# Changing the engine order of a seven-product matrix stage, and where two of its weight operands are made

## The chip, the cores and the metric

The kernel runs on one core of a Trainium2 chip. Five engines of the core work side by side, each through its own list of instructions in order: TensorE (PE, matrix products), VectorE (DVE), ScalarE (ACT), GpSimd (POOL, which here issues transfers and does little else) and SyncE (SP, which issues transfers). Engines wait for each other through semaphores. The metric is device time of one execution in microseconds; lower is better.

## The reference

Two layers of a bidirectional encoder run over 512 + 256 = 768 tokens with a model width of 1024. Each layer has a mixer, a gated convolution FFN and a small per-layer embedding. The change touches the first half of the FFN alone, in both layers:

```python
def _conv_ffn(x, w_up, conv_w, conv_b, w_down):
    u = x @ w_up
    up = jnp.pad(u, ((0, 0), (1, 1), (0, 0)))
    u = up[:, :-2] * conv_w[0] + up[:, 1:-1] * conv_w[1] + up[:, 2:] * conv_w[2] + conv_b
    a, gate = jnp.split(u, 2, axis=-1)
    return (a * jax.nn.gelu(gate, approximate=False)) @ w_down
```

`w_up` is 1024 x 5632: 22 blocks of 128 columns for `a` and 22 for `gate`.

## The kernel before

Everything is float32. A product of precision is made of three fast ones: each operand is split into a high part `hi` (ScalarE's copy to the matrix format) and a low part `lo = x - hi` (VectorE's subtraction), and the products hi*hi, hi*lo and lo*hi are added in PSUM.

For the first 4 of the 22 pairs (a block of `a` and its block of `gate`) the projection is done plainly (`proj`). The other 18 pairs go through `seven()`, a Strassen-like scheme: the 2 x 2 product of a pair's weight blocks A11, A12, A21, A22 with the halves of the input is made with seven products instead of eight. The seven weight operands, in the order in which TensorE uses them, are A11, S1 = A21 + A22, S2 = S1 + A11, S3 = A11 + A21, A12, S4 = S2 + A12 and A22. The input operands (B11, N1, N2, T3, B21, B22, N4) are made once a layer. I call one call of `seven()` "a seven", and the two stretches of 18 sevens "the seven-product stage" of layer 0 and of layer 1. Each product is 4 blocks x 3 parts = 12 matmuls of 128 x 384, so a seven has 84.

PSUM holds four accumulators a seven: x, z, y and v. TensorE writes A11 to x, S1 to z, S2 to y, S3 to v, then adds A12 to x, S4 to z and A22 to v. Before z may be written again by S4, VectorE must have read it: `u2 = y + q1` (L191, where q1 is ScalarE's copy of x, L184) and `g = z + u2` (L192; both go to the tile `ug`). VectorE also adds the results into the rows `us[0]` and `us[1]` (`u`, L1081), ScalarE copies one quarter (L1083).

After each product `after()` is called: `tick()` takes one step of the convolution and gate work of the pair before (`activate`: ScalarE's scalings L1028 and Gelu L318, VectorE's four taps L1031 and the last multiplication L1051), and `split_step()` takes one step of `split_pair`, which prepares the weights of the next seven, one operand in a step. Its loads of A21, A11, A12 and A22 come over SP's queue (L88, L89, L94; tiles `ra` and `rb`). The weight sums are made in place, in the tile that held A21 (called s) or A11 (called a), by adding transfers that GpSimd issues (`accum_op=ALU.add`): L128 makes S1 = A21 + A22 for the seven after the next, the three of L115 make S2 (`more(s, 0)`), S3 (`more(a, 2)`) and S4 (`more(s, 1)`). The splits are L110 (ScalarE, `hi`) and L111 (VectorE, `lo`); tiles `whi`/`wlo` hold S1, A11, S3 and S4, tiles `hs`/`ls` hold A12, S2 and A22. The tile that holds a and s (`ra`) has two buffers, so the loads of the seven after the next wait until S4 of the present one is split.

The order of instructions on each engine is not that of the source: a scheduler in the framework places them by its own estimate of when each is ready and of what is urgent, and the engines then run what was placed, in that order.

Of the kernel before, what the change touches and what calls it, by code (L numbers as in the profile page):

```python
# [9 lines left out]
F32 = mybir.dt.float32  # L10
F32R = mybir.dt.float32r
U8 = mybir.dt.uint8
AF = mybir.ActivationFunctionType
ALU = mybir.AluOpType
# [31 lines left out]
class Net:  # L46
# [51 lines left out]
    def split_pair(self, w):  # L98
        nc = self.nc
        src, a, s = self.ploads.pop(0)  # L100
        tiles = {}

        def parts(name, r, n, half):
            if n is None:
                hi, lo = (self.fp.tile([128, 512], F32R, tag=t, bufs=3, name=t) for t in ("hs", "ls"))
            else:
                if n not in tiles:
                    tiles[n] = [self.wp.tile([128, 1024], F32R, tag=t, bufs=2, name=t) for t in ("whi", "wlo")]
                hi, lo = [t[:, half * 512:(half + 1) * 512] for t in tiles[n]]
            nc.scalar.activation(hi, r, AF.Copy)  # L110
            nc.vector.tensor_tensor(out=lo, in0=r, in1=hi.bitcast(F32), op=ALU.subtract)  # L111
            w[name] = [(hi[:, c:c + 128], lo[:, c:c + 128]) for c in range(0, 512, 128)]

        def more(t, n):
            nc.gpsimd.dma_start(out=t, in_=src[n], accum_op=ALU.add)  # L115
        a12 = self.load_block(src[1])
        parts("S1", s, 0, 0)
        more(s, 0)
        yield
        a22 = self.load_block(src[3])  # L120
        yield
        parts("A11", a, 0, 1)
        more(a, 2)
        yield
        parts("A12", a12, None, 0)
        if self.ploads:
            after, _, t = self.ploads[0]
            nc.gpsimd.dma_start(out=t, in_=after[3], accum_op=ALU.add)  # L128
        yield
        parts("S2", s, None, 0)  # L130
        more(s, 1)
        yield
        parts("A22", a22, None, 0)
        yield
        parts("S3", a, 1, 0)
        yield
        yield
        parts("S4", s, 1, 1)
        if self.psrc:
            self.ploads.append(self.load_pair(self.psrc.pop(0)))  # L140
        elif len(self.psplits) == 1:
            self.sp += 1
            self.prep()
        yield
# [21 lines left out]
    def seven(self, c11, add):  # L166
        nc = self.nc
        X, W = self.X, self.pw.pop(0)

        def prod(bank, a, b, start):  # L170
            for n, ((wh, wl), (xh, xl)) in enumerate(zip(W[a], X[b])):
                for i, (w, v) in enumerate(((wh, xh), (wh, xl), (wl, xh))):
                    nc.tensor.matmul(bank, w, v, start=start and n == 0 and i == 0, stop=n == 3 and i == 2,  # L173
                                     skip_group_check=True)

        def after():
            self.tick()
            self.split_step()
        q1 = self.rp.tile([128, T], F32, tag="Rt", name="q1")[:, 0:HC]
        ug = self.rp.tile([128, T], F32, tag="sq", name="ug")  # L180
        u2, g = ug[:, 0:HC], ug[:, HC:T]
        x, z = self.mm()[:, 0:HC], self.mm()[:, 0:HC]
        prod(x, "A11", "B11", True)
        nc.scalar.copy(q1, x)  # L184
        after()
        prod(z, "S1", "N1", True)
        self.begin_split()
        after()
        y = self.mm()[:, 0:HC]
        prod(y, "S2", "N2", True)  # L190
        nc.vector.tensor_tensor(out=u2, in0=y, in1=q1, op=ALU.add)  # L191
        nc.vector.tensor_tensor(out=g, in0=z, in1=u2, op=ALU.add)  # L192
        after()
        v = self.mm()[:, 0:HC]
        prod(v, "S3", "T3", True)
        add(1, 1, v, g)
        after()
        prod(x, "A12", "B21", False)
        c11(x)
        after()  # L200
        prod(z, "S4", "B22", False)
        add(0, 1, z, u2)
        after()
        prod(v, "A22", "N4", False)
        add(1, 0, v, u2)
        after()

# [779 lines left out]
    def ffn(self, l):  # L989
        nc, tc, a = self.nc, self.tc, self.a  # L990
        with tc.tile_pool(name=f"f{l}", bufs=1) as fp, \
# [43 lines left out]
            def activate(j, u, negated):  # L1035
                act[j] = aslot(j, f"act{j}", F32)
                if negated:
                    c = self.hp.tile([128, AC], F32, tag="h6", name="cg")
                else:
                    c = self.rp.tile([128, AC], F32, tag="sq", name="cg")  # L1040
                gbias = conv[:, NF + j, 3:4]
                gate = conv_taps(c, u[1], *((nconv, j, gbias) if negated else (conv, NF + j, gbias)))
                lin = conv_taps(act[j], u[0], conv, j, conv[:, j, 3:4])
                next(gate), next(lin)
                yield 1
                for _ in gate:
                    yield 1
                self.other(c, c, AF.Gelu)
                for _ in lin:
                    yield 1  # L1050
                nc.vector.tensor_tensor(out=act[j], in0=act[j], in1=c, op=ALU.mult)  # L1051

            def run(gen):
                for _ in gen:
                    pass
# [5 lines left out]
            for j in range(NSTD):  # L1061
                for part in range(2):
                    n = 2 * j + part
# [5 lines left out]
                    for (c0, w), (uc, _) in zip(CH, ACOL):  # L1069
                        nc.vector.tensor_tensor(out=us[part][:, 1 + uc:1 + uc + w], in0=pj[:, c0:c0 + w],  # L1070
                                                in1=self.R[:, c0:c0 + w], op=ALU.mult)
                    if part == 1:
                        run(activate(j, us, False))
            self.drain()
            self.begin_split()
            for _ in range(6):
                self.split_step()
            for j in range(NSTD, NF):
# [6 lines left out]
                next(taps)  # L1085
                self.spawn(taps)
            self.drain()
            self.use_lnexp()
            for ph in range(2):
                accs = []  # L1090
# [7 lines left out]
                for j in range(NF):  # L1098
                    if j % 2 == 0:
                        hi, lo = self.slab()  # L1100
# [271 lines left out]
```

## Time and profile before

| | us |
|---|---|
| median of 3 runs | 2441.41 (2431.51 to 2442.25) |
| the profiled execution, its own time | 2439.16 |
| its span, first to last instruction | 2437.4 |
| seven-product stage of layer 0, from first product to the next stage's first | 332.87 |
| the same of layer 1 | 338.77 |

The profiled execution's time lies 1.8 us above its span (what lies around the instructions), and 2.3 us below the median of the runs. Stretches are given in us from the span's start. In the rows below PE is TensorE's matmul; a matmul's start is measured, its end is modelled, so the distance of starts is what counts; an instruction on another engine that is shown to take 0.69 us may be followed by the next 0.6 us after its start. "[3.49 <-DVE ug L192]" is idle time before the instruction and what ended it. The granted clock (PEclk) is the share of TensorE's full 2.4 GHz.

### The profile page before, as it was taken

Reading aid. Unit: us, or ns where it says so; the run is one execution under the profiler, and the core shown is the slowest. Engines: PE = TensorE matmul, PEld = TensorE weight load, DVE = VectorE, ACT = ScalarE, POOL = GpSimd, SP = SyncE. Lnnn points to the kernel's source line nnn. Section 1 sums busy time; section 2 is a strip of 40 time slices with the busy share of each in tenths; the row PEclk is TensorE's granted clock in tenths of the full one; section 3 lists DMA queues with packets and bytes.
Section 4 is the critical chain, followed back from the end, with each engine's and each line's share of the span. In section 5 each row is a group of like instructions: output and inputs, shape, how many; then the busy total and the mean of one; then the engine's idle time right before and its main releaser. Section 6 shows DMA issues by size and latency. Waiting matters only on the chain. (4 is left out here: it accounts for less than half of the span.)

```text
span 2437.4 us, 33498 instructions
## 1 busy us (share of the span) xinstructions
PE 2313.6 (95%) x13572; PEld 2098.2 (86%) x13572; DVE 1459.0 (60%) x2172; ACT 1036.0 (43%) x1506; POOL 193.3 (8%) x240
## 2 busy tenths in 40 slices
PE   7999999999999888889999999999998888899997
PEld 6989889898889878888888899998888887788887
DVE  7536364454568666665435687866596566664366
ACT  5333243323445334344335565545353343343353
POOL 1010010100002121110000000000021111200000
PEclk9999999999999999999999999999999999999999
DMA  4111111112336555553222211114265555531221
GB/s 158 52 53 44 53 44 44 52 44 85 110 102 133 117 110 115 109 106 102 67 74 81 97 53 36 41 38 136 100 136 114 108 106 115 101 118 61 74 87 52
DMA packets 85658, 208.74 MB, mean 86 GB/s; under 512 B 9632, under 2 KB 11680, under 8 KB 85504
## 3 DMA queue, kind: packets, MB, share of 16 engines
q1 hardware_dynamic: 60736, 162.03, 20.4%
q0 software_dynamic: 23616, 43.00, 11.7%
q8 instruction: 107, 1.75, 0.3%
q10 hardware_dynamic: 1152, 1.57, 0.2%
q14 instruction: 47, 0.39, 0.0%
HBM read 193.98 MB, written 12.58 MB: 85 GB/s over the span
## 5 line engine op out<-in xcount | busy, mean ns | idle before, releaser
L256 PE MATMUL pj<-xh,whi 128*128 128x512 f32 x2288 | 607.2, 346 | 9.1 <-ACT whi L73 6.0
L256 PE MATMUL pj<-xl,whi 128*128 128x512 f32 x2288 | 587.5, 338 | 3.5 <-DVE xl L312 3.5
L256 PE MATMUL pj<-xh,wlo 128*128 128x512 f32 x2288 | 585.7, 337 | 0.0
L256 PEld LDWEIGHTS pj<-xl,whi 128*128 128x128 f32 x2288 | 352.1, 188 | 56.0 <-DVE xl L312 5.3
L256 PEld LDWEIGHTS pj<-xh,whi 128*128 128x128 f32 x2288 | 351.1, 189 | 52.9 <-ACT whi L73 6.0
L256 PEld LDWEIGHTS pj<-xh,wlo 128*128 128x128 f32 x2288 | 349.7, 188 | 50.7
L73 ACT ACTIVATE whi<-raw 128x1024 fp32r<-128x1024 f32 (+2 forms) x182 | 181.0, 995 | 409.7 <-PE pj L256 391.5
L173 PE MATMUL mm<-x,whi 128*128 128x384 f32 x720 | 218.4, 371 | 93.6 <-DVE ug L192 90.8
L78 DVE TENSOR_TENSOR wlo<-raw,whi 128x1024 fp32r<-128x1024 f32 (+2 forms) x162 | 197.2, 1218 | 145.6 <-ACT whi L73 145.5
L173 PEld LDWEIGHTS mm<-x,whi 128*128 128x128 f32 x720 | 142.5, 207 | 106.4 <-DVE ug L192 101.2
L173 PE MATMUL mm<-x,wlo 128*128 128x384 f32 x432 | 155.5, 360 | 0.0
L110 ACT ACTIVATE whi<-ra 128x512 fp32r<-128x512 f32 x144 | 87.0, 628 | 119.7 <-DMA ra<-w_up 116.9
L173 PE MATMUL mm<-x,hs 128*128 128x384 f32 x432 | 123.0, 339 | 4.9 <-ACT q L184 4.9
L306 DVE TENSOR_TENSOR xl<-act,xh 128x772 fp32r<-128x772 f32 x88 | 83.5, 958 | 68.0 <-ACT xh L305 67.7
L115 POOL DMA_DIRECT2D ra<-w_up x108 | 104.5, 1154 | 245.1 <-DVE ls L111 188.5
L110 ACT ACTIVATE hs<-ra 128x512 fp32r<-128x512 f32 x36 | 22.7, 632 | 221.2 <-DMA ra<-w_up 209.6
L305 ACT ACTIVATE xh<-act 128x772 fp32r<-128x772 f32 x88 | 73.4, 841 | 96.8 <-PE pj L256 93.1
L111 DVE TENSOR_TENSOR ls<-ra,hs 128x512 fp32r<-128x512 f32 x36 | 24.9, 693 | 147.5 <-ACT hs L110 144.0
L111 DVE TENSOR_TENSOR wlo<-ra,whi 128x512 fp32r<-128x512 f32 x144 | 95.9, 687 | 17.3 <-ACT whi L110 16.6
L436 ACT COPY kc<-X 128x768 f32<-128x768 f32 x56 | 50.5, 902 | 124.5 <-PE mm L423 68.2
L173 PE MATMUL mm<-x,ls 128*128 128x384 f32 x288 | 97.1, 337 | 0.0
L111 DVE TENSOR_TENSOR ls<-rb,hs 128x512 fp32r<-128x512 f32 x72 | 49.5, 687 | 78.3 <-ACT hs L110 78.3
(276 smaller groups left out, 4023.7 us busy)
## 6 DMA issues: line engine op xcount, KB each, us to landing
ra<-w_up POOLq DMA_DIRECT2D x144, 256.0 KB, 4.7
raw<-w_ev SPq DMA_DIRECT2D x55, 512.0 KB, 3.5
raw<-w_dn SPq DMA_DIRECT2D x44, 512.0 KB, 3.5
rb<-w_up SPq DMA_DIRECT2D x72, 256.0 KB, 4.1
ra<-w_up SPq DMA_DIRECT2D x72, 256.0 KB, 3.4
raw<-w_od SPq DMA_DIRECT2D x24, 512.0 KB, 3.4
hd<-h SPq DMA_DIRECT2D x24, 384.0 KB, 2.3
h<-hd SPq DMA_DIRECT2D x24, 384.0 KB, 4.0
```

Of the source, the lines that this page charges most:

```text
L73: nc.scalar.activation(hi[:, s], raw[:, s], AF.Copy)
L78: nc.vector.tensor_tensor(out=lo[:, s], in0=raw[:, s], in1=hi[:, s].bitcast(F32), op=ALU.subtract)
L110: nc.scalar.activation(hi, r, AF.Copy)
L111: nc.vector.tensor_tensor(out=lo, in0=r, in1=hi.bitcast(F32), op=ALU.subtract)
L115: nc.gpsimd.dma_start(out=t, in_=src[n], accum_op=ALU.add)
L173: nc.tensor.matmul(bank, w, v, start=start and n == 0 and i == 0, stop=n == 3 and i == 2, skip_group_check=True)
L256: nc.tensor.matmul(o, w, x[:, c0:c0 + n], start=first and si == 0, stop=last and si == 2)
L305: nc.scalar.activation(xh[:, :n], src, AF.Copy)
L306: nc.vector.tensor_tensor(out=xl[:, :n], in0=src, in1=xh[:, :n].bitcast(F32), op=ALU.subtract)
L436: nc.scalar.copy(dst.rearrange("p (n c j) -> p n c j", c=2, j=h), src)
```

## The change

Three things, all within the seven-product stage.

The order: `in_order()` runs over the instructions of the stage as the source emitted them (from `begin_split()` to the last `drain()`), and ties each to the one before it on the same engine, for all engines but TensorE. No semaphore is added; the scheduler may no longer move one of them ahead of another on the same engine. TensorE's order is what it was.

S2: the adding transfer `more(s, 0)`, which was issued in the step of S1, is gone; VectorE adds a (A11, in SBUF already) to s in the step of A11.

A22: its low part is no longer VectorE's subtraction. ScalarE writes the negative of the rounded block to `lo`, and an adding transfer from DRAM adds the block.

```diff
-        def parts(name, r, n, half):
+        def parts(name, r, n, half, added=None):
...
             nc.scalar.activation(hi, r, AF.Copy)
-            nc.vector.tensor_tensor(out=lo, in0=r, in1=hi.bitcast(F32), op=ALU.subtract)
+            if added is not None:
+                nc.scalar.activation(lo, r, AF.Copy, scale=-1.0)
+                nc.gpsimd.dma_start(out=lo, in_=src[added], accum_op=ALU.add)
+            else:
+                nc.vector.tensor_tensor(out=lo, in0=r, in1=hi.bitcast(F32), op=ALU.subtract)
...
         parts("S1", s, 0, 0)
-        more(s, 0)
         yield
...
         parts("A11", a, 0, 1)
+        nc.vector.tensor_tensor(out=s, in0=s, in1=a, op=ALU.add)
         more(a, 2)
...
-        parts("A22", a22, None, 0)
+        parts("A22", a22, None, 0, 3)
...
+    def in_order(self, start):
+        last = {}
+        for i in list(self.nc.cur_bb.bb.instructions)[start:]:
+            if i.engine == mybir.EngineType.PE:
+                continue
+            if i.engine in last:
+                self.tc.add_manual_dep(i, last[i.engine].name, mybir.DependencyInfo(
+                    mybir.DependencyClass.NoSync, mybir.DependencyReason.DATA), reason="in_order")
+            last[i.engine] = i
...
             self.drain()
+            start = len(nc.cur_bb.bb.instructions)
             self.begin_split()
...
             self.drain()
+            self.in_order(start)
             self.use_lnexp()
```

VectorE, fifth seven of layer 0, from its predecessor's last addition into u1 to the first after g. Before (`cg` and `act` are taps and the last multiplication, `wlo`/`ls` low parts, `ug` u2 and then g):

```order
L1081 TENSOR_TENSOR u1_5828<-mm_7030,ug_6965 128x384
L111 TENSOR_TENSOR ls_7101<-rb_7028,hs_7100 128x512
L111 TENSOR_TENSOR wlo_7127<-ra_6881,whi_7126 128x512
L1031 SCALAR_TENSOR_TENSOR cg_7105<-u1_5828,nconv_5870,cg_7105 128x772
L1031 SCALAR_TENSOR_TENSOR act7_7104<-u0_5827,conv_5825,act7_7104 128x772
L1031 SCALAR_TENSOR_TENSOR cg_7105<-u1_5828,nconv_5870,cg_7105 128x772
L111 TENSOR_TENSOR wlo_7146<-ra_7025,whi_7145 128x512 x2
L191 TENSOR_TENSOR ug_7109<-mm_7150,q1_7108 128x384
L1051 TENSOR_TENSOR act7_7104<-act7_7104,cg_7105 128x772
L192 TENSOR_TENSOR ug_7109<-mm_7111,ug_7109 128x384
L111 TENSOR_TENSOR ls_7208<-rb_7143,hs_7207 128x512
L1081 TENSOR_TENSOR u1_5828<-mm_7174,ug_7109 128x128
```

The same place after the change (L1097 is L1081 before, L1046 is L1031, L115 is L111, L195 and L196 are L191 and L192, L126 is the new sum):

```order
L1097 TENSOR_TENSOR u1_5828<-mm_7033,ug_6969 128x384
L1046 SCALAR_TENSOR_TENSOR cg_7110<-u1_5828,nconv_5870,cg_7110 128x772
L115 TENSOR_TENSOR wlo_7132<-ra_6883,whi_7131 128x512
L1046 SCALAR_TENSOR_TENSOR cg_7110<-u1_5828,nconv_5870,cg_7110 128x772
L115 TENSOR_TENSOR wlo_7151<-ra_7028,whi_7150 128x512
L195 TENSOR_TENSOR ug_7114<-mm_7154,q1_7113 128x384
L196 TENSOR_TENSOR ug_7114<-mm_7116,ug_7114 128x384
L1046 SCALAR_TENSOR_TENSOR act7_7109<-u0_5827,conv_5825,act7_7109 128x772
L115 TENSOR_TENSOR wlo_7132<-ra_6883,whi_7131 128x512
L1097 TENSOR_TENSOR u1_5828<-mm_7178,ug_7114 128x128
```

Seven operations stood ahead of u2 and one more between u2 and g; now four stand ahead of u2 and none between. The taps on `act`, the low part of S4, that of A11 (one of the two in the row with x2) and the multiplication stand behind g.

GpSimd's transfers in the same stretch, each 256 KB. Before, in rows where a number in a tile's name tells the seven it is for:

```order
L115 DMA ra_6737<-w_up2 128x512 x3
L128 DMA ra_7025<-w_up2 128x512
L115 DMA ra_6881<-w_up2 128x512 x3
L128 DMA ra_7169<-w_up2 128x512
L115 DMA ra_7025<-w_up2 128x512 x3
```

After (L119 is `more`, L132 is L128 before, L113 is the new transfer into A22's low part):

```order
L119 DMA ra_6883<-w_up2 128x512
L132 DMA ra_7028<-w_up2 128x512
L119 DMA ra_6883<-w_up2 128x512
L113 DMA ls_7105<-w_up2 128x512
L119 DMA ra_7028<-w_up2 128x512
L132 DMA ra_7173<-w_up2 128x512
```

There are four a seven as before. S1's of the following seven (L132) now stands behind S3's of the present one (the first L119), where it used to stand first.

ScalarE in the same seven after the change (L188 is q1, L333 the Gelu, L1099 the copied quarter, L112 the new negative copy, L1043 the scalings):

```order
L188 COPY q1_7113<-mm_7115 128x384
L110 ACTIVATE whi_7131<-ra_6883 128x512
L110 ACTIVATE whi_7150<-ra_7028 128x512
L333 ACTIVATE cg_7110<-cg_7110 128x772
L110 ACTIVATE whi_7131<-ra_6883 128x512
L110 ACTIVATE whi_7150<-ra_7028 128x512
L1099 COPY u0_5827<-mm_7115 128x384
L110 ACTIVATE hs_7212<-rb_7148 128x512
L110 ACTIVATE hs_7231<-ra_7028 128x512
L110 ACTIVATE hs_7249<-rb_7176 128x512
L112 ACTIVATE ls_7250<-rb_7176 128x512
L1043 ACTIVATE cg_7255<-u1_5828,conv_5825,nconv_5870 128x772
```

In it the high parts stand in the order S3, S1 (of the next seven), then Gelu, S4, A11, the copy, A12, S2, A22: one or two for each product, as the source has them.

## Rows read from the trace of the kernel before

**Rows 1.** The page's head.

```profile
span 2437.4 us, 33498 instructions
```

**Rows 2.** The two seven-product stages: start and end, length, busy time (instructions) of PE, PEld, DVE, ACT and POOL, granted clock, DMA share, GB/s.

```profile
770.58:1103.45 332.87, 284.03 (x1515) 276.46 (x1513) 211.00 (x343) 138.60 (x222) 59.65 (x68) 0.95 0.56 114
1814.82:2153.59 338.77, 289.08 (x1515) 280.37 (x1513) 211.09 (x343) 138.83 (x222) 59.68 (x68) 0.93 0.54 112
```

**Rows 3.** TensorE's waits over the whole execution, those in the seven-product stages: us in total, times, the longest.

```profile
PE mm L173 <- DVE ug L192: 90.8, 36, 3.5
...
PE mm L173 <- ACT q L184: 4.9, 10, 0.8
...
PE mm L173 <- ACT u L1083: 2.8, 3, 1.3
```

**Rows 4.** TensorE's timeline: in layer 0's stage the starts of the first product (A11), the fourth (S3) and the fifth (A12), the first matmul behind that stage, the first of layer 1's stage and the first behind it.

```profile
770.58 0.52 PE L173 MATMUL mm<-x,whi 128*128 128x384 f32 x2
...
776.90 0.51 PE L173 MATMUL mm<-xb,whi 128*128 128x384 f32 x2
...
778.98 0.34 PE L173 MATMUL mm<-x,hs 128*128 128x384 f32 x1
...
1103.45 0.51 PE L256 MATMUL mm<-xh,whi 128*128 128x512 f32 x2
...
1814.82 0.52 PE L173 MATMUL mm<-x,whi 128*128 128x384 f32 x2
...
2153.59 0.51 PE L256 MATMUL mm<-xh,whi 128*128 128x512 f32 x2
```

**Rows 5.** TensorE's timeline around two stalls of layer 0's stage: the last A12 matmul, the first of S4 behind the wait, and a matmul 2 us behind the first stall, one 3 us and one 6 us behind the second.

```profile
946.34 0.34 PE L173 MATMUL mm<-x,ls 128*128 128x384 f32 x1
949.01 0.62 PE L173 MATMUL mm<-x,whi 128*128 128x384 f32 x2 [2.34 <-DVE ug L192]
...
951.05 0.34 PE L173 MATMUL mm<-x,wlo 128*128 128x384 f32 x1
...
964.42 0.34 PE L173 MATMUL mm<-x,ls 128*128 128x384 f32 x1
968.25 0.62 PE L173 MATMUL mm<-x,whi 128*128 128x384 f32 x2 [3.49 <-DVE ug L192]
...
971.40 0.52 PE L173 MATMUL mm<-x,wlo 128*128 128x384 f32 x1
...
974.45 0.33 PE L173 MATMUL mm<-x,wlo 128*128 128x384 f32 x1
```

**Rows 6.** VectorE's timeline ahead of and behind the first of these stalls.

```profile
943.07 1.02 DVE L1031 SCALAR_TENSOR_TENSOR cg<-u,nconv,cg 128x772 f32<-128x772 f32 x1
944.00 1.02 DVE L1031 SCALAR_TENSOR_TENSOR act<-u,conv,act 128x772 f32<-128x772 f32 x1
...
945.87 1.29 DVE L111 TENSOR_TENSOR wlo<-ra,whi 128x512 fp32r<-128x512 f32 x2
947.07 0.55 DVE L191 TENSOR_TENSOR ug<-mm,q 128x384 f32<-128x384 f32 x1
947.54 0.95 DVE L1051 TENSOR_TENSOR act<-act,cg 128x772 f32<-128x772 f32 x1
948.41 0.55 DVE L192 TENSOR_TENSOR ug<-mm,ug 128x384 f32<-128x384 f32 x1
948.88 0.68 DVE L111 TENSOR_TENSOR ls<-rb,hs 128x512 fp32r<-128x512 f32 x1
949.48 0.62 DVE L1081 TENSOR_TENSOR u<-mm,ug 128x128 f32<-128x128 f32 x2
954.80 0.69 DVE L111 TENSOR_TENSOR ls<-ra,hs 128x512 fp32r<-128x512 f32 x1 [4.71 <-ACT hs L110]
```

**Rows 7.** ScalarE's timeline behind that stall (S2's high part, S3's, and a scaling).

```profile
954.14 0.63 ACT L110 ACTIVATE hs<-ra 128x512 fp32r<-128x512 f32 x1 [6.78 <-DMA ra<-w_up]
...
955.74 0.63 ACT L110 ACTIVATE whi<-ra 128x512 fp32r<-128x512 f32 x1 [0.60 <-DMA ra<-w_up]
...
960.96 1.02 ACT L1028 ACTIVATE cg<-u,conv,nconv 128x772 f32<-128x772 f32 x1
```

**Rows 8.** GpSimd's timeline in the same seven: S1's transfer for the seven after the next, S2's and S3's, then S4's.

```profile
946.47 0.86 POOL L128 DMA_DIRECT2D ra<-w_up  x1 [9.19 <-DVE cg L1031]
947.01 2.10 POOL L115 DMA_DIRECT2D ra<-w_up  x2
955.79 0.86 POOL L115 DMA_DIRECT2D ra<-w_up  x1 [6.68 <-DVE ls L111]
```

**Rows 9.** The transfers of L115 (S2, S3, S4): issue time on GpSimd, and from issue to landing.

```profile
L115 POOL DMA_DIRECT2D ra<-w_up x108: 862/1214/1604, 766.4 to 2136.4; - x108
...
DMA to landing us min/median/max: 3.9/6.2/8.8
```

**Rows 10.** The same of L128 (S1).

```profile
L128 POOL DMA_DIRECT2D ra<-w_up x34: 862/862/908, 763.3 to 2111.5; - x34
...
DMA to landing us min/median/max: 3.9/4.1/6.8
```

**Rows 11.** Two operations: ScalarE's negative copy of a block, which the plain projections have, and the subtraction of a low part (ns min/median/max).

```profile
L75 ACT ACTIVATE wlo<-raw x20: 614/616/617, 721.4 to 1800.4; 128x512 fp32r<-128x512 f32 x20
...
L111 DVE TENSOR_TENSOR ls<-rb,hs x72: 679/687/693, 649.4 to 2141.7; 128x512 fp32r<-128x512 f32 x72
```

## The prediction

> **What bounds the kernel now.** I read the page first, then the stretches by stage, then TensorE's waits, then the timelines of one seven. The span is 2437.4 us [rows 1], and TensorE hardly ever waits outside the two seven-product stages. Inside them it does: they take 332.87 and 338.77 us, at a granted clock of 0.95 and 0.93 [rows 2]. What they would take without a wait is read from the first products: four of them start within 778.98 - 770.58 = 8.40 us [rows 4], so one takes 2.10, a seven 14.70 and eighteen 264.6 us. Both stages together are therefore 68.3 + 74.2 = **142.4 us** longer than TensorE's own work.
>
> Where they go: 36 waits, one a seven, on VectorE's L192 (g) take 90.8 us; waits on two copies of ScalarE take 4.9 and 2.8 [rows 3], 98.5 in all. The rest is clock: (1 - 0.95) x 332.87 + (1 - 0.93) x 338.77 = 40.3 us [rows 2]. Behind a wait of 3.49 us the matmuls last 0.52 instead of 0.34 us, which is the level of 1.2 GHz instead of 2.4; behind 2.34 us they stay at 0.34 [rows 5]. Together 138.8 of the 142.4; I put the last 3.6 down to restarts.
>
> Why g is late: S2's product ends some 4.2 us, two products, before the last A12 matmul at 946.34 [rows 5], at about 942.3, and g needs two half-microsecond additions behind it. But VectorE works through taps and low parts from 943.07 to 947.07 before it comes to u2, and through the last multiplication (947.54) before g at 948.41 [rows 6]. TensorE starts S4 at 949.01 [rows 5]. VectorE isn't short of time: 211.00 us of work in eighteen sevens [rows 2] is 11.7 of 14.70 a seven. It stands idle 4.71 us afterwards, for S2's high part [rows 6], which ScalarE starts only when S2's adding transfer has landed, after 6.78 us of idling [rows 7]. So the order on VectorE and one late transfer make the stall.
>
> **The change part by part.** *Removed and added work.* VectorE loses 36 subtractions of 0.687 us [rows 11] and gains 36 sums; no row shows a float32 sum of that size in place, and I take the subtraction's price, having the same shape and two operands from the same memory. Bounds: the half-size additions' 0.55 and the tap's 1.02 [rows 6]. Net 0, at the most 36 x 0.33 = 12 us, in VectorE's 3 us of slack a seven. ScalarE gains 36 copies of 0.616 us [rows 11], 22 us in all, on an engine that is busy 138.60 of 332.87 us [rows 2]. GpSimd issues as many transfers as before. All of this is hidden as long as the order lets it be.
>
> *The order, walked through one seven* (0 is the start of A11's product; products end at 2.1, 4.2, 6.3, 8.4, 10.5, 12.6 and 14.7; durations from rows 6, 7 and 11). ScalarE begins with A22's high part and negative copy when the last A22 product has ended (1.3), then two scalings of 0.93 from start to start (3.2), q1 (3.6), S3's high part (4.2), and S1's when the S1 product has freed its buffer (4.9). VectorE: tap 2.3 to 3.3, S3's low part 4.9, tap 5.8, S1's low part 6.4, then u2 at the end of S2's product, 6.5, and g ready at 7.5. S4's product starts at 10.5, **3.0 us behind g**, where it now waits 2.5 on average. Its own low part is done at 9.1, the addition into u1 at 9.6, the next tap 10.5, A11's low part 11.1, the weight sum 11.8, the multiplication 12.7, A12's low part 13.3, the addition into u0 13.8 and S2's low part 14.4, ahead of the next A22 product's end. S2's high part no longer waits for a transfer. No step of TensorE finds its operand late, so the waits of rows 3 go, and the clock's loss with them.
>
> *What could come round late.* Since VectorE's order is fixed, a late transfer holds everything behind it. The longest cycle goes through S1's transfer (L132), which on GpSimd now stands behind S3's, which waits for the weight sum. From the issue of S3's: 0.54 to the next issue [rows 8], the transfer's time L, S1's high part 0.63, low part 0.60, u2 and g 0.94, tap 0.93, S4's low part 0.60, addition 0.53, tap 0.93, A11's low part 0.60, weight sum 0.69 and 0.30 from VectorE's end to GpSimd's start (954.80 + 0.69 to 955.79) [rows 6 to 8]: **L + 7.3 us**. A transfer that goes alone lands after 4.1 us [rows 10], the middle one of L115, often second in a bunch, after 6.2, the slowest after 8.8 [rows 9]. Second in a bunch of two close issues is what L132 will be, so I take 6.2: 13.5 us, under 14.70 by 1.2. The cycle decides only from L = 7.4 on; at 8.8 it is 16.1. S4's cycle, by the same rows, is L + 7.0, and its issue comes 2 us behind L132's.
>
> A rule speaks against the change here. The Trainium skill ("SBUF — State Buffer", section "SBUF: two separate sides") says that VectorE and GpSimd share a port pair under an exclusive lock, that some VectorE operations take it, and that a transfer issued by GpSimd then can't get its descriptors written. By that rule, if the operations here are of that kind, S3's and S1's issues would each wait for the running one and the sum would be that of rival (b); by the row they don't wait: L128's issue at 946.47 took 0.86 us in the middle of two-operand subtractions, like that at 955.79 [rows 6, 8].
>
> *The ends of a stage.* In the first seven the Gelu of the plain pair stands behind S4's and A11's high parts on ScalarE, hence behind S4's transfer, and VectorE's multiplication for it ahead of u2; a third transfer in a bunch would make g about 2 us late. At the end, SP loads three rows of h ahead of the second weight slab of the next stage. Each has a bound of 0 and of 3.5 us, the longest wait seen [rows 3]; I take 2 and 1 us in each stage, 6 in all.
>
> *Sum.* 2439.2 - 142.4 + 6 = 2302.8 us for the profiled execution; the median of the runs lies 2.3 higher, so **2305 us**. A measurement of this kernel tells about 0.5%, 12 us, from no change.
>
> **The rivals.** *(a) The transfers bound the sevens.* For it: the DMA share is already 0.56 of 332.87 us [rows 2], 10.4 us a seven, which is 70% of 14.70; and S3's, S1's, S4's and A22's transfers come within some 4 us. Against it: the same number as before in a bunch of three and one. With L of 8.1 to 8.8 a seven takes 15.4 to 16.1 us, and 36 x 0.7 to 1.4 = 25 to 50 us of the gain are lost: 2330 to 2355.
>
> *(b) VectorE's running operation holds up GpSimd's issues.* Each of the two issues of the cycle waits for a tap of at most 1.02 us [rows 6]: the cycle is 15.5, 0.8 over, and 36 x 0.8 = 29 us are lost: 2334. The issue of 0.86 us amid VectorE's work speaks against it [rows 6, 8]. This is what the Trainium skill's rule above would do.
>
> *(c) The wait only changes its name.* TensorE's S4 needs S4's low part as well as g. If S4's transfer lands so late that the seven stays near its present (332.87 + 338.77) / 36 = 18.66 us, nothing is gained: L + 7.0 = 18.66 needs 11.7 us, against 8.8 seen. Time 2430 to 2452.
>
> *(d) Slower, by the cycle through S1's transfer.* In the fixed order VectorE cannot go on to u2 and g while S1's part is missing, which the scheduler's order could arrange. It ends above no change by 12 us when L + 7.3 exceeds 18.66 + 0.34, that is from L = 11.7 us; at 13 us, half as long again as the slowest now, a seven takes 20.3 and the kernel 2441 + 36 x 1.64 = 2500 us. Against it: none of 142 adding transfers took over 8.8 [rows 9, 10].
>
> **How the numbers follow.** The forecast 0.59, with its own range 2290 to 2318; (a) 0.24; (b) 0.06; (c) 0.05; (d) 0.06. The likeliest case gives 2305. Downwards nothing goes beyond the whole 142.4 us except the spread of the runs, whose lowest is 9.9 under the median: 2441.4 - 142.4 - 9.9 = 2289, so 2290. Upwards (a) and (b) are taken in: 2358. Faster: the first three, 0.89; same 0.05; slower 0.06.
>
> **What would show it.** Stages of 265 to 270 us at a granted clock near 1.00; no wait on the line of g; VectorE's multiplication behind g; S2's high part not waiting for a transfer; transfers of S1 landing in 6 to 7 us. The prediction is wrong if TensorE waits at S4's or S3's product for a low part, or if VectorE idles for S1's high part and that for a transfer, with sevens over 15 us: then (a). A sum of 36 gains that leaves the total unchanged would speak for a new stall at the stage's ends, which I price at 6 us.

## The result, and the profile after

The changed kernel takes a median of **2297.73 us** (2295.33 to 2298.36, three runs) against 2441.41 before: a ratio of 0.9421, interval 0.9382 to 0.9459, 143.7 us less. The forecast was 2305, with a range of 2290 to 2358.

The page's head of the profiled execution, whose own time is 2298.36 us, with the busy time of the engines and the chain that ended last by engine:

```profile
span 2296.5 us, 33387 instructions
...
PE 2271.8 (99%) x13572; PEld 2071.2 (90%) x13572; DVE 1460.1 (64%) x2172; ACT 1059.1 (46%) x1542; POOL 192.7 (8%) x240
...
PE 97%; DVE 2%; ACT 1%; DMA 0%; issue 0%; POOL 0%; SPq 0%; DVEq 0%; ACTq 0%
```

The two seven-product stages, in the columns of [rows 2]:

```profile
771.73:1036.14 264.41, 264.41 (x1514) 264.35 (x1513) 208.43 (x338) 147.28 (x235) 60.22 (x69) 1.00 0.68 146
1748.03:2012.42 264.39, 264.39 (x1515) 264.39 (x1513) 208.81 (x339) 147.43 (x236) 60.21 (x69) 1.00 0.68 146
```

TensorE is busy for the whole of each stage, at a granted clock of 1.00. A seven takes 264.4 / 18 = 14.69 us, where it took 18.66. The stages lost (332.87 - 264.41) + (338.77 - 264.39) = 142.84 us; the span lost 140.9, so the rest of the kernel is 1.9 us longer.

TensorE's waits, the whole list, in the columns of [rows 3]:

```profile
PE pj L271 <- ACT whi L73: 6.2, 1, 6.2
PE mm L401 <- DVE acc L385: 3.6, 1, 3.6
PE pj L271 <- DVE xh L324: 3.1, 1, 3.1
PE pj L271 <- DVE xl L327: 2.4, 2, 1.9
PE mm L271 <- DVE u L1097: 0.3, 1, 0.3
```

No line of `seven()` (L177) is among them: 98.5 us of waits in the stages have become none.

VectorE's timeline in one seven of layer 0, u2 and g, then the new sum and the last multiplication:

```profile
837.42 0.55 DVE L195 TENSOR_TENSOR ug<-mm,q 128x384 f32<-128x384 f32 x1
838.01 0.56 DVE L196 TENSOR_TENSOR ug<-mm,ug 128x384 f32<-128x384 f32 x1
...
842.08 0.69 DVE L126 TENSOR_TENSOR ra<-ra 128x512 f32<-128x512 f32 x1
842.68 0.95 DVE L1066 TENSOR_TENSOR act<-act,cg 128x772 f32<-128x772 f32 x1
```

ScalarE's in the same seven: S2's high part, then S1's of the next seven, and S4's and A11's together:

```profile
842.80 0.63 ACT L110 ACTIVATE hs<-ra 128x512 fp32r<-128x512 f32 x1
...
850.42 0.63 ACT L110 ACTIVATE whi<-ra 128x512 fp32r<-128x512 f32 x1 [1.29 <-DMA ra<-w_up]
...
852.04 1.16 ACT L110 ACTIVATE whi<-ra 128x512 fp32r<-128x512 f32 x2 [0.25 <-DMA ra<-w_up]
```

GpSimd's transfers, S3's and behind it S1's of the next seven:

```profile
843.45 0.87 POOL L119 DMA_DIRECT2D ra<-w_up  x1 [9.77 <-ACT hs L110]
844.03 1.19 POOL L132 DMA_DIRECT2D ra<-w_up  x1
```

And all of S1's transfers, in the columns of [rows 10]:

```profile
L132 POOL DMA_DIRECT2D ra<-w_up x34: 862/1177/1207, 770.5 to 1981.3; - x34
...
DMA to landing us min/median/max: 4.4/5.6/7.0
```

The reader is to see that the multiplication stands behind g, that S2's high part waits for no transfer, that S1's high part for the next seven now stands ahead of S4's, and that S1's transfer, which landed after a median of 4.1 us when it went first [rows 10], lands after 5.6.

### The profile page after: what moved, and what is told of

The parts are those of the page before. It is cut to its first block, busy times and chain, and to the rows that moved or that the text cites. A ratio compares the mean times of both kernels' runs of the same rounds, so it can differ in the third digit from the quotient of the medians.

```text
span 2296.5 us, 33387 instructions
## 1 busy us (share of the span) xinstructions
PE 2271.8 (99%) x13572; PEld 2071.2 (90%) x13572; DVE 1460.1 (64%) x2172; ACT 1059.1 (46%) x1542; POOL 192.7 (8%) x240
## 4 chain that ended last, share of the span: by engine, by line
PE 97%; DVE 2%; ACT 1%; DMA 0%; issue 0%; POOL 0%; SPq 0%; DVEq 0%; ACTq 0%
PE pj L271 52%; PE mm L177 23%; PE mm L271 12%; PE mm L438 4%; PE mm L520 2%; PE mm L881 1%; PE mm L488 1%; PE mm L424 1%; PE mm L742 0%; PE mm L798 0%; PE mm L874 0%; DVE y L1196 0%; PE mm L401 0%; PE mm L479 0%; PE mm L533 0%
## 5 line engine op out<-in xcount | busy, mean ns | idle before, releaser
L177 PE MATMUL mm<-x,whi 128*128 128x384 f32 x720 | 196.4, 338 | 0.0
L177 PE MATMUL mm<-x,wlo 128*128 128x384 f32 x432 | 145.7, 337 | 0.0
L177 PEld LDWEIGHTS mm<-x,whi 128*128 128x128 f32 x720 | 131.4, 188 | 0.1
L177 PE MATMUL mm<-x,hs 128*128 128x384 f32 x432 | 121.7, 336 | 0.0
L115 DVE TENSOR_TENSOR wlo<-ra,whi 128x512 fp32r<-128x512 f32 x144 | 98.5, 685 | 29.7 <-ACT whi L110 29.6
L1046 DVE SCALAR_TENSOR_TENSOR cg<-u,nconv,cg 128x772 f32<-128x772 f32 x72 | 73.4, 1019 | 50.1 <-ACT cg L1043 50.1
L177 PE MATMUL mm<-x,ls 128*128 128x384 f32 x288 | 97.2, 337 | 0.0
L119 POOL DMA_DIRECT2D ra<-w_up x72 | 62.8, 873 | 385.8 <-ACT hs L110 332.5
L271 PE MATMUL mm<-xh,whi 128*128 128x512 f32 x352 | 90.5, 337 | 0.3 <-DVE u L1097 0.3
L271 PE MATMUL mm<-xl,whi 128*128 128x512 f32 x352 | 90.6, 337 | 0.0
```

The lines of the kernel that those rows point to most:

```text
L271: nc.tensor.matmul(o, w, x[:, c0:c0 + n], start=first and si == 0, stop=last and si == 2)
L1046: nc.vector.scalar_tensor_tensor(out=c, in0=u[:, i:i + AC], scalar=w[:, f, i:i + 1], in1=c, op0=ALU.mult, op1=ALU.add)
```

## The experiments

Every kernel here computes the whole reference; each was timed in three rounds beside the kernel before, which took 2433 to 2438 us on those chips. The first set takes the change apart. The theories when it was written: **O**, the stall is where u2 and g stand in VectorE's order, and the order alone cures it; **C**, the stall comes from S2's late adding transfer, behind which VectorE idles and then works in a bunch, and S2's sum on VectorE cures it; **B**, VectorE has too much work. A seven's mean length below is both stages' length over 36.

| run | what it has of the change | median us | ratio (interval) | a seven, us |
|---|---|---|---|---|
| order_alone | order | 2296.78 | 0.9445 (0.9429 to 0.9461) | 14.69 |
| s2_alone | S2 | 2325.12 | 0.9564 (0.9547 to 0.958) | 15.51 |
| a22_alone | A22 | 2455.04 | 1.0101 (1.0079 to 1.0122) | 18.99 |
| s2_a22_no_order | S2 and A22 | 2314.94 | 0.9522 (0.9504 to 0.9541) | 15.14 |
| order_s2 | order and S2 | 2297.14 | 0.9435 (0.9406 to 0.9463) | 14.69 |
| order_a22 | order and A22 | 2297.05 | 0.9432 (0.9403 to 0.946) | 14.69 |
| order_vector_only | order on VectorE alone | 2326.23 | 0.955 (0.9521 to 0.9579) | 15.50 |
| order_scalar_only | order on ScalarE alone | 2296.71 | 0.9423 (0.9402 to 0.9444) | 14.69 |
| s4_behind_s1 | one tie on ScalarE | 2308.03 | 0.9485 (0.9463 to 0.9508) | 14.98 |

**The order alone** (order_alone), in the changed kernel:

```diff
         parts("S1", s, 0, 0)
+        more(s, 0)
...
-        nc.vector.tensor_tensor(out=s, in0=s, in1=a, op=ALU.add)
...
-        parts("A22", a22, None, 0, 3)
+        parts("A22", a22, None, 0)
```

> The kernel before with the source order on all engines but TensorE; S2 stays an adding transfer and A22's low part VectorE's subtraction. Theory O (the stall is where u2 and g stand on VectorE): g is ready 3 us ahead of S4's product, sevens of 14.7 us, 2295 to 2310 us. Theory C (the stall is S2's late adding transfer, for which VectorE idles 4.7 us and then has everything to do at once): the transfer is still there, and VectorE still waits for S2's high part ahead of the rest: 2380 to 2440 us.

Measured 2296.78 us: the whole gain. C's figure is out.

**S2 on VectorE alone** (s2_alone): `self.in_order(start)` is left out and A22 as before, the sum stays.

```diff
-        parts("A22", a22, None, 0, 3)
+        parts("A22", a22, None, 0)
...
-            self.in_order(start)
```

> The kernel before with S2 made by VectorE, the order left to the scheduler. On VectorE five to seven operations still stand ahead of u2, and the new sum stands between u2 and g. Theory O: the wait on g stays, 2400 to 2440 us. Theory C: VectorE no longer idles for S2, works ahead, g is in time though it stands late in the row: 2295 to 2330 us.

Measured 2325.12 us: 4.36% of the 5.55% that the order brings. O's figure is out too: the one cures all of it and the other four fifths, without each other, although the scheduler again put taps and low parts ahead of u2, and the sum between u2 and g. Both theories lacked what the two have in common.

**A22's transfer alone** (a22_alone): without `in_order`, S2 by its transfer.

```diff
         parts("S1", s, 0, 0)
+        more(s, 0)
...
-        nc.vector.tensor_tensor(out=s, in0=s, in1=a, op=ALU.add)
...
-            self.in_order(start)
```

> The kernel before with A22's low part by ScalarE's negative copy and an adding transfer, order and S2 as before. VectorE has 0.6 us less to do in a seven. Theories O and C: the wait on g stays but for that, at most 36 x 0.6 = 22 us, 2415 to 2441 us. A theory B (VectorE has too much to do) would have it at 2380 or lower.

Measured 2455.04 us, 1.0% slower, which I had not expected; the ring below shows where the time may lie.

**Pairs** (s2_a22_no_order, order_s2, order_a22): from the changed kernel one part is taken away, the order, A22's transfer or S2's sum.

```diff
-            self.in_order(start)
```

> The changed kernel without the source order: both operands as after the change, the order left to the scheduler. Taps, low parts and the sum stand ahead of u2, the last multiplication between u2 and g. Theory O: 2400 to 2440 us. Theory C: 2295 to 2320 us.

```diff
-        parts("A22", a22, None, 0, 3)
+        parts("A22", a22, None, 0)
```

> Source order and S2 by VectorE, A22's low part by VectorE's subtraction as before: 36 subtractions of 0.69 us more on VectorE than after the change. Theories O and C: the same as the changed kernel, 2295 to 2303 us, the subtraction falling into VectorE's wait for ScalarE's scaling at the start of a seven. Theory B: up to 36 x 0.6 = 22 us slower, 2320 us.

```diff
         parts("S1", s, 0, 0)
+        more(s, 0)
...
-        nc.vector.tensor_tensor(out=s, in0=s, in1=a, op=ALU.add)
```

> Source order and A22 by an adding transfer, S2 by an adding transfer as before: five adding transfers a seven instead of four. Theory O: no stall from VectorE; 2295 to 2310 us if five transfers fit in 14.7 us. If the transfers bound the sevens, 36 x 1 to 2 us more, 2335 to 2370. Theory C: 2380 to 2440 us.

With the order in place neither operand moves the time (2296.8 to 2297.7 us for all four). Without it, the two together give 2314.94 us, 10 us better than S2 alone, although A22's transfer alone made the kernel slower. B is out: order_alone has 212.1 us of VectorE work a stage, more than the 211.0 of before [rows 2], and no wait.

**What the two cures share: a ring.** The kernel before has to be read over a whole period, from one S2 transfer to the next. [Rows 6 to 8] hold the first half; the second half is from ScalarE's, VectorE's and GpSimd's timelines of the kernel before (S4's high part, q1, and S1's and A11's high parts of the next seven; A22's low part, S4's and the first of three taps, then S1's and A11's low parts; S1's transfer for a later seven, then S2's and S3's), and one line of SyncE's, the load that this S1's transfer adds to:

```profile
959.90 0.63 ACT L110 ACTIVATE whi<-ra 128x512 fp32r<-128x512 f32 x1 [2.61 <-DMA ra<-w_up]
...
961.89 0.45 ACT L184 COPY q<-mm 128x384 f32<-128x384 f32 x1
962.25 1.15 ACT L110 ACTIVATE whi<-ra 128x512 fp32r<-128x512 f32 x2
...
961.09 0.69 DVE L111 TENSOR_TENSOR ls<-rb,hs 128x512 fp32r<-128x512 f32 x1 [2.27 <-ACT hs L110]
961.70 0.68 DVE L111 TENSOR_TENSOR wlo<-ra,whi 128x512 fp32r<-128x512 f32 x1
962.30 1.01 DVE L1031 SCALAR_TENSOR_TENSOR cg<-u,nconv,cg 128x772 f32<-128x772 f32 x1
...
965.10 1.29 DVE L111 TENSOR_TENSOR wlo<-ra,whi 128x512 fp32r<-128x512 f32 x2
...
962.41 0.33 SPq L88 DMA_DIRECT2D ra<-w_up  x1
...
965.84 0.86 POOL L128 DMA_DIRECT2D ra<-w_up  x1 [9.19 <-DVE wlo L111]
966.38 2.11 POOL L115 DMA_DIRECT2D ra<-w_up  x2
```

S2's transfer is issued at 947.01 [rows 8] and ScalarE starts S2's high part at 954.14 [rows 7]: 7.13 us. S4 is made in S2's buffer, so its transfer waits for S2's low part and is issued at 955.79: 1.65. ScalarE starts S4's high part at 959.90: 4.11. In the scheduler's order A22's high part, a scaling and q1 stand behind that, and only then S1's and A11's for the next seven, at 962.25: 2.35. VectorE's order has S4 ahead of S1 too: A22's and S4's low parts and three taps run without a pause from 961.09, and S1's low part comes only at 965.10, 2.2 us after its high part was done. On GpSimd S2's transfer stands behind S1's for a later seven, which needs the buffer that S4's low part frees and the load into it. The next S2 transfer leaves at 966.38: 4.13. The steps add up to 19.37 us, which is the distance of the two issues by construction; TensorE's two starts of S4 at that place are 968.25 - 949.01 = 19.24 us apart [rows 5]. What makes the steps a chain is that each was released by the one before or stood behind it on its engine. So two adding transfers one behind the other, closed into a ring because S4's parts stand ahead of S1's of the next seven, in three queues at once (high parts on ScalarE, low parts on VectorE, the transfer behind the load on GpSimd), set the period of 18 to 19 us. That g was late is how TensorE noticed.

In the source, S1's high and low parts stand ahead of S4's, and S2's transfer ahead of S1's for the later seven, so the order cuts the ring. S2's sum on VectorE leaves it, but takes out a transfer. S2's ring in s2_alone, on VectorE, ScalarE and GpSimd (the sum, S4's transfer, S4's high part, the next sum):

```profile
886.67 0.69 DVE L126 TENSOR_TENSOR ra<-ra 128x512 f32<-128x512 f32 x1
...
890.73 0.86 POOL L119 DMA_DIRECT2D ra<-w_up  x1 [1.97 <-DVE ls L115]
...
894.91 0.63 ACT L110 ACTIVATE whi<-ra 128x512 fp32r<-128x512 f32 x1 [1.45 <-DMA ra<-w_up]
...
901.77 0.68 DVE L126 TENSOR_TENSOR ra<-ra 128x512 f32<-128x512 f32 x1
```

This turn takes 901.77 - 886.67 = 15.10 us, just over TensorE's 14.69; the stages' mean is 15.51. And a22_alone, on ScalarE, VectorE and GpSimd (S4's high part; S1's and A11's low parts; S1's transfer for a later seven, then S2's and S3's):

```profile
946.01 0.63 ACT L110 ACTIVATE whi<-ra 128x512 fp32r<-128x512 f32 x1 [2.52 <-DMA ra<-w_up]
...
950.64 1.29 DVE L115 TENSOR_TENSOR wlo<-ra,whi 128x512 fp32r<-128x512 f32 x2
...
952.09 0.87 POOL L132 DMA_DIRECT2D ra<-w_up  x1 [3.23 <-DVE wlo L115]
952.62 2.12 POOL L119 DMA_DIRECT2D ra<-w_up  x2
```

The new negative copy stands on ScalarE between S4's high part and S1's, but it does not lengthen the ring there: from S4's high part to S1's low part it is 950.64 - 946.01 = 4.63 us, against 965.10 - 959.90 = 5.20 before, since A22's low part is gone from VectorE. What is longer is the way from S1's low part to S2's transfer, 952.62 - 950.64 = 1.98 against 966.38 - 965.10 = 1.28, behind S1's transfer for the later seven; and the transfers of S2, S3 and S4 land after a median of 6.7 us, against 6.2 [rows 9]. In these rows and medians that comes to some 0.6 us more, where a seven grew by 18.99 - 18.66 = 0.33 us on the average; none of it was tried apart, so the cause stays open in part.

**Which engine's order** (order_vector_only): order_alone, with the ties on VectorE only; order_scalar_only is the same with ScalarE.

```diff
-            if i.engine == mybir.EngineType.PE:
+            if i.engine != mybir.EngineType.DVE:
                 continue
```

> The source order tied on VectorE alone; ScalarE, GpSimd and SyncE left to the scheduler, S2 and A22 as in the kernel before. GpSimd's and SyncE's order comes out as with all engines tied, ScalarE's differs. Theory O: the place of u2 and g on VectorE is what counts, 2295 to 2320 us. If ScalarE's order counts as well, 2340 us or more, with VectorE waiting for high parts.

Measured 2326.23 us, between the two figures that I wrote, with u2 and g back to back as in the source and 17.3 us of waits, now on a low part. So VectorE's order alone brings four fifths of the gain. In ScalarE's order S4's high part still stands ahead of q1 and of S1's, and a seven takes 15.50 us.

> The order of the source on ScalarE alone; VectorE's is the scheduler's, S2 is a transfer and A22's low part VectorE's, as before. VectorE's own order again puts a low part between u2 and g and two taps on act, one low part more than in the source, ahead of u2. If what counts is where u2 and g stand on VectorE, the waits on g stay for the most part and it comes to 2400 to 2440 us, as far above the order on VectorE alone (2326) as that was under before. If what counts is that no engine holds its later work behind S2's late transfer (in ScalarE's order of before S2's high part stands ahead of the copy, S4's or A11's high part and a scaling; in the order of the source it stands behind them), ScalarE's order gives most of it: 2297 to 2340 us, with waits on g of 20 to 30 us in all. The first half of the bunch being pulled forward by 1.6 us of ScalarE's work, I expect 2310 to 2335.

Measured 2296.71 us, the whole gain and under the 2310 to 2335 that I expected, with no wait in the stages. VectorE's timeline in it (a tap, u2, a low part, g):

```profile
836.02 1.02 DVE L1046 SCALAR_TENSOR_TENSOR act<-u,conv,act 128x772 f32<-128x772 f32 x1
836.95 0.55 DVE L195 TENSOR_TENSOR ug<-mm,q 128x384 f32<-128x384 f32 x1
837.42 0.68 DVE L115 TENSOR_TENSOR wlo<-ra,whi 128x512 fp32r<-128x512 f32 x1
838.02 0.55 DVE L196 TENSOR_TENSOR ug<-mm,ug 128x384 f32<-128x384 f32 x1
```

A tap and a low part stand where the source doesn't have them, and g starts at the same time as in the changed kernel (838.01), whose stage began 0.4 us later, so that here it comes 0.4 us later in its seven. The low part between u2 and g is S4's: with ScalarE tied, the scheduler put it behind S1's on VectorE too.

**One tie** (s4_behind_s1), in the kernel before. It sets the ring against the prediction's reading, since as many of VectorE's operations as before stand ahead of u2 and g.

```diff
-            nc.scalar.activation(hi, r, AF.Copy)
+            i = nc.scalar.activation(hi, r, AF.Copy)
+            if name == "S1":
+                self.s1 = i.ins
+            if name == "S4":
+                self.tc.add_manual_dep(i.ins, self.s1.name, mybir.DependencyInfo(
+                    mybir.DependencyClass.NoSync, mybir.DependencyReason.DATA), reason="s4_behind_s1")
```

> The kernel before with one tie and nothing else of the change: on ScalarE, S4's high part must stand behind S1's high part of the next seven, where the scheduler had it ahead of the copy q1, S1's and A11's. VectorE's order still has all four taps, S4's low part and the last multiplication ahead of u2, and one low part between u2 and g. Cycle theory: what sets the seven's length is a ring through two adding transfers, S2's transfer, S2's high and low part, S4's transfer, S4's high part, then by ScalarE's order S1's high part of the next seven and, with its low part, the next S2's transfer; the tie cuts the ring, and the time falls to 2297 to 2310 us, with waits on g under 10 us in all. Place theory: what counts is how much of VectorE's work stands ahead of u2 and g; that is as much as before, and the time stays at 2400 to 2441 us with waits on g of 70 to 95 us.

Measured 2308.03 us: 5.15% of the 5.77% that ScalarE's whole order brings. Three views follow: TensorE's wait on g (L197 here) over the whole execution; VectorE's timeline from the last multiplication to g; GpSimd's, with S2's transfer at two turns and S4's between (L120 is L115 before):

```profile
PE mm L178 <- DVE ug L197: 7.4, 5, 2.4
```

```profile
882.71 0.95 DVE L1056 TENSOR_TENSOR act<-act,cg 128x772 f32<-128x772 f32 x1
883.58 0.55 DVE L196 TENSOR_TENSOR ug<-mm,q 128x384 f32<-128x384 f32 x1
884.05 0.68 DVE L116 TENSOR_TENSOR wlo<-ra,whi 128x512 fp32r<-128x512 f32 x1
884.65 0.55 DVE L197 TENSOR_TENSOR ug<-mm,ug 128x384 f32<-128x384 f32 x1
```

```profile
882.48 0.86 POOL L120 DMA_DIRECT2D ra<-w_up  x1 [7.38 <-DVE wlo L116]
...
888.94 0.87 POOL L120 DMA_DIRECT2D ra<-w_up  x1 [1.62 <-DVE ls L116]
896.96 0.86 POOL L120 DMA_DIRECT2D ra<-w_up  x1 [7.14 <-DVE wlo L116]
```

All taps and the multiplication stand ahead of u2 and a low part ahead of g, the same number of operations ahead of g as before, and the 36 waits of 90.8 us [rows 3] are 5 of 7.4. S2's transfers come 14.48 us apart here. The one tie did not leave the other queues as they were: the scheduler put S4's low part behind S1's on VectorE, and S1's transfer for the later seven behind S2's and S3's on GpSimd. So the run shows that the ring is cut where S4 stands behind S1, and that the amount of work ahead of g is not the cause; of the three places, ScalarE's by itself still holds a seven at 15.50 us (order_vector_only); for the other two no run tells. The largest two of the waits left, 2.35 and 2.27 us, are in the last seven of each stage.

**Where the margin lies** (g_late, s1_late, s1_later), all in the changed kernel. g_late emits u2 and g behind the step of the pair before instead of ahead of it:

```diff
-        nc.vector.tensor_tensor(out=u2, in0=y, in1=q1, op=ALU.add)
-        nc.vector.tensor_tensor(out=g, in0=z, in1=u2, op=ALU.add)
         after()
+        nc.vector.tensor_tensor(out=u2, in0=y, in1=q1, op=ALU.add)
+        nc.vector.tensor_tensor(out=g, in0=z, in1=u2, op=ALU.add)
```

> The changed kernel with u2 and g emitted one step later: a tap on act and S4's low part stand ahead of u2. By the walk g is ready at 9.1 us of a seven instead of 7.5, still 1.4 us ahead of S4's product at 10.5: no change, 2295 to 2301 us. If g has no such margin, 36 x 1.5 = 54 us slower, 2350 us.

Measured 2296.9 us (2295.05 to 2297.49) and one wait of 0.4 us on g: of the walk's 3.0 us at least the 1.6 of this step (from 7.5 to 9.1) were really spare. s1_late issues S1's transfer (the three lines with `self.ploads`) behind S4's, as shown; s1_later puts the same lines behind `parts("A22", ...)`:

```diff
-        if self.ploads:
-            after, _, t = self.ploads[0]
-            nc.gpsimd.dma_start(out=t, in_=after[3], accum_op=ALU.add)
         yield
         parts("S2", s, None, 0)
         more(s, 1)
+        if self.ploads:
+            after, _, t = self.ploads[0]
+            nc.gpsimd.dma_start(out=t, in_=after[3], accum_op=ALU.add)
         yield
         parts("A22", a22, None, 0, 3)
         yield
```

> The changed kernel with S1's adding transfer (for the seven after the next) issued one step later, behind S4's. The cycle through it gets longer by the work from the weight sum to S2's low part: L + 9.9 us instead of L + 7.3; with the L of 5.6 us that the changed kernel shows 15.5, 0.8 over TensorE's 14.7. The 3 us by which g is early are used up first: 2 x (18 x 0.8 - 3) = 23 us slower, 2315 to 2335 us. If transfers are hidden whenever they come: 2297 us.

Measured 2343.25 us (ratio 0.9628, 0.9612 to 0.9645), 8 us above my range, with a seven of 15.98, where L + 9.9 with the 5.8 us that the transfer takes here (median) gives 15.7: the ring through S1's transfer is there, and it decides once it stands one place later.

> The same transfer issued two steps later, behind A22's. It is then issued at about 2.3 us of the next seven, S1's high part starts at 8, S1's low part, u2, g, a tap and S4's low part follow, and S4's low part is ready at 11.6 where its product would start at 10.5: TensorE waits 1.1 us in each seven at S4, for S4's low part and not for g, 36 x 1.1 = 40 us slower, 2330 to 2345 us. If transfers are hidden: 2297 us.

Measured 2391.69 us (ratio 0.9823, 0.9805 to 0.9842), a seven of 17.40, far above what I wrote. The ring in its trace: S1's transfer (L137) at two turns with S4's and A22's ahead of it, S1's high part, S1's low part, S2's low part:

```profile
894.58 1.18 POOL L137 DMA_DIRECT2D ra<-w_up  x1
...
900.32 0.63 ACT L110 ACTIVATE whi<-ra 128x512 fp32r<-128x512 f32 x1 [3.87 <-DMA ra<-w_up]
...
900.98 0.69 DVE L115 TENSOR_TENSOR wlo<-ra,whi 128x512 fp32r<-128x512 f32 x1 [2.87 <-ACT whi L110]
...
908.86 0.68 DVE L115 TENSOR_TENSOR ls<-ra,hs 128x512 fp32r<-128x512 f32 x1
...
909.83 0.86 POOL L119 DMA_DIRECT2D ra<-w_up  x1 [1.50 <-DVE ls L115]
911.28 0.88 POOL L113 DMA_DIRECT2D ls<-w_up  x1 [0.58 <-ACT ls L112]
911.86 1.21 POOL L137 DMA_DIRECT2D ra<-w_up  x1
```

5.74 to S1's high part, 0.66 to its low part, 7.88 of VectorE's fixed order to S2's low part, 0.97 to S4's issue, 1.45 to A22's, which waits for the negative copy, and 0.58 to S1's: 17.28 us. The issue had moved past two waits of GpSimd's queue, and both are in the period; I had left the ring out and counted only TensorE's wait for S4's low part.

## Why the prediction was right, step by step

- *Ideal and excess.* 14.70 us a seven, 264.6 a stage and an excess of 142.4 us: measured 264.4 and 142.84. Counting waits plus clock gave 138.8, so the 3.6 us put down to restarts were real excess too.
- *The clock.* 0.95 and 0.93 became 1.00 with the waits gone.
- *Why g was late: the step that failed.* "So the order on VectorE and one late transfer make the stall" named a part of it. The late transfer was rightly seen; that two such transfers follow each other in a ring, closed by S4's parts ahead of S1's, was not. The work that stands ahead of u2 and g, which the prediction blamed, is not what holds TensorE up: with as much of it there and one tie on ScalarE the time is 2308 us. VectorE's order does count, but as a part of the ring: with the source's order on VectorE and ScalarE's left to the scheduler the time is 2326, and the waits are no longer on g. The 6.78 us that ScalarE idled [rows 7] were a step of the ring, and I read the 4.71 us that VectorE idled as something that came after the stall, when the next stall grew out of it. The forecast stood because the walk used the new order of all engines, with S1's high part ahead of S4's, and so had the cut in it without naming it; and whatever takes the waits away ends at TensorE's own 14.69 us a seven, so the time alone can't tell the two readings apart. In that the right time owes something to luck.
- *Prices.* The sum in place takes 0.68 to 0.69 us, as taken. S1's transfer, taken at 6.2 us, has a median of 5.6 and at most 7.0, under the 7.4 from which it decides. From the sum's end to GpSimd's issue went 843.45 - (842.08 + 0.69) = 0.68 us instead of 0.30. A22's and S2's parts, costed at nothing, are worth nothing beside the order.
- *The ends of a stage.* 6 us taken, none found in the stages; the rest of the kernel grew by 1.9. With a profiled execution that lay 0.6 us above the median instead of 2.3 below, that is the whole miss: (6 - 142.4) - (1.9 - 142.8) = 4.5, and 2.9, against 7.3 measured.
- *Rival (a)* had its price but not its condition: no transfer of S1 reached 7.4 us. s1_late and s1_later show what it would have been like, with 46 and 94 us lost.
- *Rival (b).* S3's issue started at 843.45 inside VectorE's multiplication (842.68 to 843.63), so it did not wait for the running operation. The Trainium skill ("SBUF — State Buffer", section "SBUF: two separate sides") states the lock on descriptors for VectorE's operations in a two-port mode, and names a float32 copy as one. This row shows no such lock for a multiplication of two tiles. The median issue of L132 is 1.18 us instead of 0.86, which costs nothing here.
- *Rivals (c) and (d).* No wait took the place of g's, and no seven came near 18.7 us.

## What to carry to other kernels

Where a pipelined stage has a period longer than its main engine's work, follow one period round, through data and through places in every queue, until the sum gives the period that the trace shows; the instruction that the main engine waits for is only where the ring is met. Such a ring is cut by moving one piece of work past another in the queues that close it, or shortened by taking a transfer out of it, and here the second cure was worth nothing once the first was in. One tie can move work on other engines as well, where a scheduler places it anew: read every queue again before a cause is named. With a fixed order, each place that a transfer's issue is moved back in its queue can cost the waits that it passes.

## What the runs showed that I had not expected

With the same five adding transfers a seven, those of L119 (S2's, S3's and S4's) land in 3.8/4.8/6.8 us (least, median, most) in order_a22, where they leave at a steady pace and the DMA share is 0.81 in the stage of layer 0, and in 3.9/6.7/8.9 us in a22_alone, where two are issued back to back and the share is 0.62: how late a transfer lands went with how the issues are bunched, not with how much is moved. And S2's sum without the order leaves 27.4 us on the table, which the order on VectorE alone (28.5 us) does too, while one tie on ScalarE leaves 10.3.
